# An encoder step with 16 attention heads: which projection blocks are computed beside the attention

## The chip, the cores and the metric

The kernel is one program on one core of a Trainium2 chip. The metric is the device time in microseconds (us). The engines are named as in the profile: PE is TensorE (matmuls; PEld its weight loads), DVE is VectorE, ACT is ScalarE, POOL is GpSimd, and SP issues most of the transfers.

## The reference, cut to what matters

Two groups of requests, 512 prompt rows and 8 x 16 sample rows, go through one layer together, 640 rows in all:

```python
h = rms_norm(x, g_pre)
(sq, sk, sv, sg, bq, bk, bv, bg, mq, mg, gsb, gbd, gmm) = split(h @ w_in)   # 13312 columns
o_sb = stick_breaking(sq, sk, sv)        # 6 heads of 128; sigmoid and a running product
o_bd = band_attention(bq, bk, bv, bias)  # 6 heads; softmax with a bias
o_mm = memory_attention(mq, mk, mv)      # 4 heads; softmax over 256 memory rows
merged = (sigmoid(gsb) * ((o_sb * silu(sg)) @ w_up_sb)
          + sigmoid(gbd) * ((o_bd * silu(bg)) @ w_up_band)
          + sigmoid(gmm) * ((o_mm * silu(mg)) @ w_up_mem))
y = x + rms_norm(merged @ w_out, g_post)
```

The sample rows attend to cached keys and values as well, 512 rows per stream (256 for the memory heads).

## The kernel before, in words

The 13312 columns of `w_in` are 104 blocks of 128 columns: 24 for the six stick-breaking heads (q, k, v, gate), 24 for the six band heads, 8 for the four memory heads (q, gate), and 48 merge gates (3 x 16). Every product is done as three matmuls of split operands (high x high, high x low, low x high), so a plain block is 16 k-steps x 3 x 2 halves of the rows = 96 matmuls of 128x320. Two blocks can also be done together with seven half-size products in place of eight: such a pair (`block_pair`) is 7 x 8 x 3 = 168 matmuls.

The stages are, in time: the memory projection and the norm of x; four plain gate blocks (`gate`); 34 pairs; the attention with 32 plain blocks beside it; the three up-projections (`up`); the output projection with the last norm.

- The pairs are 12 for the band heads' q, k, v and gate, whose results go to DRAM (`put_raw`, issued by POOL, tensors `raw_d`), and 22 for merge gates, whose sigmoids go to DRAM (`put_gate`, issued by ACT, tensors `sig_d`). Between the pairs SP lays the cached keys out anew in DRAM (`cut_keys`, tensors `keys_d`).
- In the attention the heads follow `ORDER`. 0 to 5 are stick-breaking, 6 to 11 band, 12 to 15 memory heads. A stick-breaking or memory head computes its own blocks as plain ones (`transposed`, `head_g`, both over `x_proj`), 24 + 8 = 32 blocks; a band head loads its four (`loaded`). The generators of a head are run in turns (`interleave`): the prompt's attention, the sample's scores, and the sample's output of the head before.
- The prompt's attention of a head has four query blocks. For each, PE computes scores `s`; DVE and ACT turn them into weights `b` (softmax for band and memory heads, `softmax`; two sigmoids and a running product for stick-breaking heads, `stick`); PE transposes `b` into `tp`; ACT and DVE split `tp` into `wth` and `wtl`; PE multiplies these with the values into `o`.
- The plain blocks take their weights in half blocks of 512 KB (`load_w`, tile `wr`), which ACT and DVE split into `wh` and `wl`.

The order of the program's text is not the order on the engines: a scheduler orders all instructions of each engine when the program is built, by its own estimate of their times. `tc.issue_after(x)` holds what stands in it behind the instruction x on the same engine; `x_proj` uses it to keep the plain blocks in the order of the text. Once built, each engine runs its list strictly in that order, and waits at an instruction whose inputs are not there.

ACT holds one set of functions at a time. Where an exponential follows a sigmoid, or the other way round, an ACT_TABLE_LOAD stands between them in ACT's list; the build puts it there.

Of the kernel before, what the change touches and what calls it, by code (L numbers as in the profile page):

```python
# [8 lines left out]
F32 = mybir.dt.float32  # L9
F32R = mybir.dt.float32r  # L10
AF = mybir.ActivationFunctionType
ALU = mybir.AluOpType
# [4 lines left out]
P = 128  # L17
# [18 lines left out]
LATE = 4  # L36

FIRST = 4


ORDER = (0, 6, 1, 7, 12, 2, 8, 3, 9, 13, 4, 5, 14, 15, 10, 11)

# [4 lines left out]
def stream_step_kernel(  # L47
# [46 lines left out]

    raw_d = [[dpool.tile([P, NT], F32, name=f"raw_d{n}_{h}") for h in range(6)] for n in range(4)]
    sig_d = [dpool.tile([P, NT], F32, name=f"sig_d{i}") for i in range(3 * KB)]
# [77 lines left out]

    def proj(w, col, kn, src, acc, half=8, back=False):

        starts = range(0, kn, half)
        for i0, k0 in enumerate(reversed(starts) if back else starts):
            n = min(half, kn - k0)
            wh, wl = load_w(w[k0 * P:(k0 + n) * P, col:col + P].rearrange("(k p) c -> p k c", p=P), [P, n, P])  # L180
            for k in range(n):
                bh, bl = src(k0 + k)
                first, last = i0 == 0 and k == 0, i0 == len(starts) - 1 and k == n - 1
                for a, b, f, l in ((wh, bh, True, False), (wh, bl, False, False), (wl, bh, False, True)):
                    for s in range(2):
                        PE.matmul(acc[:, s, :HF], a[:, k], b[s],  # L186
                                  start=first and f, stop=last and l)

    def x_proj(col, acc):

        nonlocal last_mm, back
        with tc.issue_after(last_mm or last_on(PE)):
            proj(w_in, col, KB, x_src, acc, back=back)
        last_mm, back = last_on(PE), False

# [175 lines left out]
    def loaded(n, h):  # L371
        t = pa.tile([P, NT], F32, tag=f"l{n}", name=f"l{n}", bufs=2 if n == 0 else 1)
        SP.dma_start(t, raw_d[n][h])
        return t

    def transposed(col, n, raw):

        if raw is not None:
            return loaded(n, raw)
        acc = new_acc()  # L380
        x_proj(col, acc)
        t = pa.tile([P, NT], F32, tag=f"l{n}", name=f"l{n}", bufs=2 if n == 0 else 1)
        ACT.copy(halves(t), acc[:, :, :HF])
        return t

    def head_g(col, raw=None):
        sg = stg.tile([P, NT], F32, tag="sig", name="sg")
        if raw is not None:
            SP.dma_start(sg, raw_d[3][raw])
            return sg  # L390
        acc = new_acc()
        x_proj(col, acc)
        ACT.activation(halves(sg), acc[:, :, :HF], AF.Sigmoid)
        DVE.tensor_tensor(halves(sg), acc[:, :, :HF], halves(sg), op=ALU.mult)  # L394
        return sg
# [205 lines left out]
    def causal_head(i):  # L601

        kind, h, c0 = ("sb", i, C_SB) if i < 6 else ("bd", i - 6, C_BD)
        cv = (cache_sb_v, cache_band_v)[i // 6]
        kp, vp, ks, vs = (tokens(t)[:, h] for t in ((sbk_p, sbv_p, sbk_s, sbv_s), (bdk_p, bdv_p, bdk_s, bdv_s))[i // 6])
        strip, strips = None, None
        if kind == "bd":
# [10 lines left out]
            strips = (st[:, TS:], st2)  # L618
        raw = h if kind == "bd" else None
        sg = head_g(c0 + 2304 + h * P, raw)  # L620
        vt = transposed(c0 + 1536 + h * P, 2, raw)
        nat = pa.tile([P, 4, P], F32, tag="nat", name="nat")
# [5 lines left out]
        vn = natural_new(vt, vs, "vn")  # L628
        qt = transposed(c0 + h * P, 0, raw)
        kt = transposed(c0 + 768 + h * P, 1, raw)  # L630
        v = split_v(nat)
# [18 lines left out]
    def mem_head(h):  # L650
        vn = pa.tile([P, 4, P], F32, tag="nat", name="vnm")[:, :2]
        kn = pa.tile([P, NT], F32, tag="l2", name="knm")[:, :NMEM].rearrange("p (t e) -> p t e", t=2)
        for t, o in ((kn, 0), (vn, 512)):
            SP.dma_start(t, kv_d[:, o + h * P:o + (h + 1) * P].rearrange("(t p) e -> p t e", p=P))
        qt = transposed(C_MM + h * P, 0, None)
        sg = head_g(C_MM + 512 + h * P)
        tp = bank("tp")
# [24 lines left out]

    def gate(i):
        acc = new_acc()
        x_proj(C_GATE + i * P, acc)
# [29 lines left out]
    for i in range(FIRST):  # L715
        gate(i)
        third.append(sums(2 * i))
# [122 lines left out]
    with tc.tile_pool(name="att", bufs=1, reuse_waits="tile") as pa:  # L840
        qm, wTm = zero_padded(4)

        rest = iter(())
        for h in ORDER:
            prompt, score, out = causal_head(h) if h < 12 else mem_head(h - 12)
            interleave(rest, prompt, score)
            rest = out
        interleave(rest)
    xs.close()
# [19 lines left out]
    def up(i):  # L869
# [132 lines left out]
```

## Time and profile before

| | us |
|---|---|
| median of 3 runs (2084.43 to 2088.02) | 2087.05 |
| the profiled execution, its own time | 2088.03 |
| its span in the profile | 2086.3 |
| PE busy | 2045.1 (98%) |
| DVE busy | 1104.4 (53%) |
| ACT busy | 817.0 (39%) |
| POOL busy | 570.1 (27%) |

A row of groups gives line, engine, operation, out<-in by the program's names, shapes and count, then busy time, mean ns of one, and idle time of the engine before them with what ended it. PE's busy time is a union of matmuls whose ends are modelled; what PE loses is seen in its waits and in the granted clock (PEclk). A row of waits reads: who <- for whom: us in total, times, longest us.

### The profile page before, as it was taken

To read this page: it belongs to the slowest core of one execution; us is meant where nothing else is said; L and a number is where in the kernel's file an instruction comes from. 1 tells how busy PE (TensorE), PEld (TensorE's weight loads), DVE (VectorE), ACT (ScalarE), POOL (GpSimd) and SP (SyncE) were. 2 spreads that over 40 slices of the span, in tenths; PEclk is the share of its full clock that TensorE was granted. 3 is DMA by queue.
4 is the path that set the end of the run, shared out by engine and by line. 5 is a ranking of instruction groups with operands and counts; after the bars stand their busy time and mean duration, and the time that the engine had idled before them with its cause. 6 is when DMAs were issued, how large, how long until landed. Compare 5 with 4: busy or idle time off the path is not lost.

```text
span 2086.3 us, 35971 instructions
## 1 busy us (share of the span) xinstructions
PE 2045.1 (98%) x13997; PEld 1934.7 (93%) x13997; DVE 1104.4 (53%) x1804; ACT 817.0 (39%) x1567; POOL 570.1 (27%) x539
## 2 busy tenths in 40 slices
PE   7999999999999999999999999989999999999998
PEld 5999999999999999999999799979998899998886
DVE  6875555555555555555355645555455665542234
ACT  6543444444444444444233333333334232322221
POOL 1155455664444444441010101010100015330000
PEclk9999999999999999999999999989999999999999
DMA  7656665565556655645557646653556875532225
GB/s 264 213 145 157 166 162 146 140 154 147 147 138 162 164 140 136 154 127 167 154 157 214 186 131 197 195 177 109 164 156 216 242 205 172 166 124 72 81 89 214
DMA packets 556889, 336.49 MB, mean 161 GB/s; under 512 B 271761, under 2 KB 507297, under 8 KB 555181
## 3 DMA queue, kind: packets, MB, share of 16 engines
q1 hardware_dynamic: 542942, 294.53, 50.9%
q0 software_dynamic: 6864, 23.93, 3.3%
q10 hardware_dynamic: 6912, 15.73, 2.0%
q8 instruction: 110, 1.80, 0.4%
q14 instruction: 61, 0.50, 0.1%
HBM read 288.75 MB, written 76.35 MB: 175 GB/s over the span
## 4 chain that ended last, share of the span: by engine, by line
PE 91%; DMA 2%; issue 2%; DVE 2%; POOL 1%; ACT 1%; SPq 0%; DVEq 0%; POOLq 0%; ACTq 0%
PE q L748 40%; PE acc L186 32%; PE ya L171 4%; PE ya L172 3%; PE ya L173 3%; PE s L528 2%; POOL merged L888 1%; PE o L587 1%; DMA kc<-keys_d 1%; DMA wr<-in_w_mem_kv_dram 1%; PE tp L458 1%; PE o L171 1%; DMA or<-osg_d 0%; PE o L172 0%; PE o L173 0%
## 5 line engine op out<-in xcount | busy, mean ns | idle before, releaser
L115 DVE TENSOR_TENSOR wl<-wr,wh 128x512 fp32r<-128x512 f32 (+1 forms) x524 | 383.0, 734 | 384.0 <-ACT wh L114 373.3
L114 ACT CAST wh<-wr 128x512 fp32r<-128x512 f32 (+1 forms) x524 | 316.7, 608 | 607.4 <-PE acc L186 250.5
L115 DVE TENSOR_TENSOR wl<-ws,wh 128x512 fp32r<-128x512 f32 x272 | 231.3, 852 | 232.4 <-ACT wh L114 231.8
L748 PE MATMUL q<-xh,wh 128*128 128x320 f32 x1088 | 336.2, 309 | 0.0
L748 PE MATMUL q<-xh,wl 128*128 128x320 f32 x1088 | 336.2, 309 | 0.0
L748 PE MATMUL q<-xl,wh 128*128 128x320 f32 x1088 | 336.1, 309 | 0.0
L114 ACT CAST wh<-ws 128x512 fp32r<-128x512 f32 x272 | 168.9, 622 | 271.3 <-PE q L748 230.3
L186 PE MATMUL acc<-xh,wl 128*128 128x320 f32 x1152 | 269.9, 312 | 0.0
L186 PE MATMUL acc<-xh,wh 128*128 128x320 f32 x1152 | 267.5, 311 | 1.2 <-DVE sg L394 1.2
L186 PE MATMUL acc<-xl,wh 128*128 128x320 f32 x1152 | 267.7, 311 | 0.0
L748 PE MATMUL q<-th,wl 128*128 128x320 f32 x816 | 252.2, 309 | 0.0
L748 PE MATMUL q<-th,wh 128*128 128x320 f32 x816 | 252.1, 309 | 0.0
L748 PE MATMUL q<-tl,wh 128*128 128x320 f32 x816 | 252.1, 309 | 0.0
L748 PEld LDWEIGHTS q<-xh,wl 128*128 128x128 f32 x1088 | 204.6, 188 | 0.0
L748 PEld LDWEIGHTS q<-xl,wh 128*128 128x128 f32 x1088 | 204.5, 188 | 0.0
L748 PEld LDWEIGHTS q<-xh,wh 128*128 128x128 f32 x1088 | 204.5, 188 | 0.0
L186 PEld LDWEIGHTS acc<-xh,wh 128*128 128x128 f32 x1152 | 193.2, 188 | 8.1 <-issue 5.4
L186 PEld LDWEIGHTS acc<-xl,wh 128*128 128x128 f32 x1152 | 193.5, 188 | 7.6 <-issue 7.5
L186 PEld LDWEIGHTS acc<-xh,wl 128*128 128x128 f32 x1152 | 193.9, 188 | 2.3 <-issue 1.8
L741 POOL TENSOR_TENSOR ws<-wr 128x512 f32<-128x512 f32 x102 | 150.7, 1491 | 93.7 <-DVE wl L115 77.1
L748 PEld LDWEIGHTS q<-th,wl 128*128 128x128 f32 x816 | 153.2, 188 | 0.2 <-DVE wl L115 0.2
L748 PEld LDWEIGHTS q<-tl,wh 128*128 128x128 f32 x816 | 153.2, 188 | 0.0
(239 smaller groups left out, 3262.2 us busy)
## 6 DMA issues: line engine op xcount, KB each, us to landing
wr<-in_w_in_dram SPq DMA_DIRECT2D x208, 512.0 KB, 4.7
kc<-keys_d SPq DMA_DIRECT2D x48, 512.0 KB, 5.0
wr<-in_w_out_dram SPq DMA_DIRECT2D x32, 512.0 KB, 3.7
sig_d<-sig ACTq DMA_DIRECT2D x48, 320.0 KB, 5.3
sig<-sig_d SPq DMA_DIRECT2D x48, 320.0 KB, 3.7
keys_d<-in_cache_sb_k_dram SPq DMA_DIRECT2D x96, 128.0 KB, 4.5
keys_d<-in_cache_band_k_dram SPq DMA_DIRECT2D x96, 128.0 KB, 4.5
vc<-in_cache_sb_v_dram SPq DMA_DIRECT2D x48, 256.0 KB, 5.5
```

The costliest lines, as they stand in the source:

```text
L114: ACT.copy(hi, src)
L115: DVE.tensor_tensor(lo, src, hi.bitcast(F32), op=ALU.subtract)
L171: PE.matmul(out, ah, bh, start=start, stop=False)
L172: PE.matmul(out, ah, bl, start=False, stop=False)
L173: PE.matmul(out, al, bh, start=False, stop=stop)
L186: PE.matmul(acc[:, s, :HF], a[:, k], b[s], start=first and f, stop=last and l)
L458: PE.transpose(tp[:, kb * P:(kb + 1) * P], b[:, kb * P:(kb + 1) * P], ident)
L528: return PE.matmul(s[32 * j:32 * j + 32, :nc_], qm[:, j, par * 32:par * 32 + 32], kts[j], start=par == 0, stop=par == 1, tile_position=(0, ...
L587: PE.matmul(o[32 * j:32 * j + 32, :P], l, r, start=i == 0, stop=i == len(steps) - 1, tile_position=(0, 32 * j))
L741: eng.tensor_tensor(o, a[c], b[c], op=op)
L748: PE.matmul(bank_, a[:, k], b[:, k], start=first and k == 0 and n == 0, stop=k == KH - 1 and n == 2, skip_group_check=not first)
L888: POOL.tensor_tensor(merged[:, j], merged[:, j], sig, op=ALU.add)
```

## The change

It has five parts.

1. All 16 heads load their blocks from DRAM. The pairs are now 12 for the band heads, 12 for the stick-breaking heads, 4 for the memory heads, and 6 for merge gates: 34 again.
2. The 32 plain blocks beside the attention are merge gates. `x_proj` becomes a generator (`x_proj_steps`) that hands over after each half block. One half block is run ahead of each head, and `beside(PER)` runs four more in turns with the head's own generators; 64 half blocks are used up within the 13th head.
3. The gate of a head has a tile of its own (`sg`, two buffers), and q has one buffer in place of two.
4. `ORDER` has the memory heads later: 0, 6, 1, 7, 2, 8, 3, 9, 4, 12, 5, 13, 14, 10, 15, 11.
5. In the up-projections the tiles `or` and `sig` share four buffers in place of five.

The number of pairs (34) and of plain blocks (36) is the same, and so are the heads' own matmuls.

```diff
-ORDER = (0, 6, 1, 7, 12, 2, 8, 3, 9, 13, 4, 5, 14, 15, 10, 11)
+ORDER = (0, 6, 1, 7, 2, 8, 3, 9, 4, 12, 5, 13, 14, 10, 15, 11)
...
-    def x_proj(col, acc):
+    def x_proj_steps(col, acc):
 
         nonlocal last_mm, back
-        with tc.issue_after(last_mm or last_on(PE)):
-            proj(w_in, col, KB, x_src, acc, back=back)
-        last_mm, back = last_on(PE), False
+        steps, back = proj_steps(w_in, col, KB, x_src, acc, 8, back), False
+        for _ in range(KB // 8):
+            with tc.issue_after(last_mm or last_on(PE)):
+                next(steps)
+            last_mm = last_on(PE)
+            yield
...
-        t = pa.tile([P, NT], F32, tag=f"l{n}", name=f"l{n}", bufs=2 if n == 0 else 1)
+        t = pa.tile([P, NT], F32, tag=f"l{n}", name=f"l{n}")
         SP.dma_start(t, raw_d[n][h])
         return t
...
-        sg = head_g(c0 + 2304 + h * P, raw)
-        vt = transposed(c0 + 1536 + h * P, 2, raw)
+        sg = head_g(i)
+        vt = loaded(2, i)
...
-        qt = transposed(c0 + h * P, 0, raw)
-        kt = transposed(c0 + 768 + h * P, 1, raw)
+        qt, kt = loaded(0, i), loaded(1, i)
...
-    pairs = [(C_BD + 768 * n + h * P, put_raw(n, h)) for n in range(4) for h in range(0, 6, 2)]
-    pairs += [(C_GATE + i * P, put_gate(i)) for i in range(FIRST, 3 * KB, 2)]
+    gates = [*range(KB), *range(2 * KB, 3 * KB), *range(KB, 2 * KB)]
+    pairs = [(c + 768 * n + h * P, put_raw(n, i + h)) for c, i in ((C_BD, 6), (C_SB, 0)) for n in range(4) for h in range(0, 6, 2)]
+    pairs += [(C_MM + 512 * n + h * P, put_raw(3 * n, 12 + h)) for n in range(2) for h in range(0, 4, 2)]
+    pairs += [(C_GATE + i * P, put_gate(i)) for i in gates[FIRST:-BESIDE:2]]
...
-        for h in ORDER:
+        left = gates[-BESIDE:]
+        steps = (None for i in left for _ in gate_steps(i))
+
+        def beside(n):
+
+            for _ in range(n):
+                yield
+                next(steps, None)
+                yield
+                yield
+
+        for n, h in enumerate(ORDER):
+            next(steps, None)
             prompt, score, out = causal_head(h) if h < 12 else mem_head(h - 12)
-            interleave(rest, prompt, score)
+            interleave(rest, prompt, score, beside(PER))
             rest = out
+        for _ in steps:
+            pass
         interleave(rest)
...
-        r = po.tile([P, NT], F32, tag="sig", name="or", bufs=5)
+        r = po.tile([P, NT], F32, tag="sig", name="or", bufs=4)
...
-        sig = po.tile([P, NT], F32, tag="sig", name="sig", bufs=5)
+        sig = po.tile([P, NT], F32, tag="sig", name="sig", bufs=4)
```

Three places show the order on the engines; a number behind a name tells one tile from the next. The first is PE's list in band head 9, from the transposes of the first query block's weights (`b_14797`) to the first product with the values. In the kernel before these rows follow each other:

```order
L458 MATMUL tp_14847<-ident_66,b_14797 128x128 x4
L593 MATMUL t3_14856<-ident_66,on_14845 128x128
L171 MATMUL s_14860<-kh_14745,qh_14738 128x384
L172 MATMUL s_14860<-kl_14746,qh_14738 128x384
L173 MATMUL s_14860<-kh_14745,ql_14739 128x384
L458 MATMUL tp_14875<-ident_66,b_14864 128x128 x3
L171 MATMUL o_14883<-wth_14789,vh_14734 128x256
```

The same place in the changed kernel (second query block, weights `b_14821`):

```order
L174 MATMUL s_14817<-kh_14640,qh_14633 128x384
L175 MATMUL s_14817<-kl_14641,qh_14633 128x384
L176 MATMUL s_14817<-kh_14640,ql_14634 128x384
L189 MATMUL acc_14754<-xh11_80,wh_14860 128x320
...
L189 MATMUL acc_14960<-xh01_76,wh_14963 128x320
L454 MATMUL tp_14832<-ident_66,b_14821 128x128 x3
L189 MATMUL acc_14960<-xl00_75,wh_14963 128x320
```

Before, the scores `s_14860` are followed at once by the transposes of the weights made of them, and those at once by the product that needs their split; now 49 matmuls of a gate block stand between the scores and the transposes, and 24 between the transposes and the product.

The second place is ACT's list in the same band head. Before, from the first query block's exponential to the third's:

```order
L569 COPY wTm_10604<-tp_14778 128x16x2x16
L481 ACT_TABLE_LOAD
L481 ACTIVATE b_14797,sm_14799<-b_14797,sm_14799 128x512
L590 COPY on_14845<-o_14784 128x128
L114 CAST wth_14789<-tp_14847 128x4x128
L481 ACTIVATE b_14864,sm_14866<-b_14864,sm_14866 128x384
L114 CAST wth_14789<-tp_14875 128x3x128
L393 ACT_TABLE_LOAD
L393 ACTIVATE sg_15412<-acc_15413 128x640
L481 ACT_TABLE_LOAD
L481 ACTIVATE b_14909,sm_14911<-b_14909,sm_14911 128x256
```

Now, from the same exponential on:

```order
L565 COPY wTm_10634<-tp_14673 128x16x2x16
L477 ACT_TABLE_LOAD
L477 ACTIVATE b_14692,sm_14694<-b_14692,sm_14694 128x512
...
L477 ACTIVATE b_14821,sm_14823<-b_14821,sm_14823 128x384
L117 CAST wh_15053<-wr_15047 128x512
L680 ACT_TABLE_LOAD
L680 ACTIVATE sig_14957<-acc_14754 128x640
L674 DMA sig_d18_197<-sig_14957 128x640
L117 CAST wth_14684<-tp_14832 128x3x128
L117 CAST wh_15111<-wr_15109 128x512
L477 ACT_TABLE_LOAD
```

In each of the heads 6 to 9 a merge gate's sigmoid now stands between the second and third exponentials, and another ahead of the sample's, each with a table load on either side; before, only heads 7 and 9 have one sigmoid each among their exponentials (that of a memory head's gate). From the end of the pairs to the last softmax ACT's list has 15 table loads before and 37 now: 19 ahead of an exponential, 14 ahead of a gate's sigmoid, 4 ahead of a stick-breaking head's sigmoid.

The third place is SP's list at the start of the attention. Before, behind the last load of the pairs:

```order
L141 DMA wr_10786<-in_w_in_dram 128x8x128
L514 DMA kc_11144<-keys_d0_90 128x1024
L514 DMA kc_11171<-keys_d0_90 128x1024
L141 DMA wr_10860<-in_w_in_dram 128x8x128
L609 DMA strip_11278<-rext_d_82 128x512
```

and now:

```order
L144 DMA wr_10988<-in_w_in_dram 128x8x128
L390 DMA sg_10696<-raw_d3_0_163 128x640
L385 DMA l2_10698<-raw_d2_0_151 128x640
L385 DMA l0_10713<-raw_d0_0_123 128x640
L385 DMA l1_10715<-raw_d1_0_139 128x640
L510 DMA kc_10764<-keys_d0_90 128x1024
```

Head 0's gate, v, q and k are loaded first there, ahead of its keys. On PE, 48 matmuls of the first gate block stand between the last pair and the transposes of v (`l2`); before, two plain blocks and 27 matmuls of a third stood ahead of the first such transposes.

More of the change, by code (lines that the diff above doesn't have):

```diff
@@ L36 @@
 LATE = 4
+BESIDE = 32
+PER = 4
 FIRST = 4
-ORDER = (0, 6, 1, 7, 12, 2, 8, 3, 9, 13, 4, 5, 14, 15, 10, 11)
+ORDER = (0, 6, 1, 7, 2, 8, 3, 9, 4, 12, 5, 13, 14, 10, 15, 11)
 C_SB, C_BD, C_MM, C_GATE = 0, 3072, 6144, 7168
@@ L93, in stream_step_kernel @@
     b12_d = dpool.tile([P, KH, HF], F32, name="b12_d")
-    raw_d = [[dpool.tile([P, NT], F32, name=f"raw_d{n}_{h}") for h in range(6)] for n in range(4)]
+    raw_d = [[dpool.tile([P, NT], F32, name=f"raw_d{n}_{h}") if n in (0, 3) or h < 12 else None for h in range(16)]
+             for n in range(4)]
     sig_d = [dpool.tile([P, NT], F32, name=f"sig_d{i}") for i in range(3 * KB)]
@@ L173, in mm3, with proj_steps @@
         PE.matmul(out, al, bh, start=False, stop=stop)
-    def proj(w, col, kn, src, acc, half=8, back=False):
+    def proj_steps(w, col, kn, src, acc, half=8, back=False):
         starts = range(0, kn, half)
@@ L187, in proj @@
                                   start=first and f, stop=last and l)
-    def x_proj(col, acc):
-        nonlocal last_mm, back
-        with tc.issue_after(last_mm or last_on(PE)):
-            proj(w_in, col, KB, x_src, acc, back=back)
-        last_mm, back = last_on(PE), False
+            yield
+    def proj(*args):
+        for _ in proj_steps(*args):
+            pass
+    def x_proj_steps(col, acc):
+        nonlocal last_mm, back
+        steps, back = proj_steps(w_in, col, KB, x_src, acc, 8, back), False
[4 more added lines that the diff above has]
+            yield
     def x_src(k):
@@ L371, in loaded, with head_g @@
     def loaded(n, h):
-        t = pa.tile([P, NT], F32, tag=f"l{n}", name=f"l{n}", bufs=2 if n == 0 else 1)
+        t = pa.tile([P, NT], F32, tag=f"l{n}", name=f"l{n}")
         SP.dma_start(t, raw_d[n][h])
         return t
[L376 to L394, printed above, removed]
+    def head_g(h):
+        sg = pa.tile([P, NT], F32, tag="sg", name="sg", bufs=2)
+        SP.dma_start(sg, raw_d[3][h])
         return sg
@@ L601, in causal_head @@
     def causal_head(i):
-        kind, h, c0 = ("sb", i, C_SB) if i < 6 else ("bd", i - 6, C_BD)
+        kind, h = ("sb", i) if i < 6 else ("bd", i - 6)
         cv = (cache_sb_v, cache_band_v)[i // 6]
@@ L618, in causal_head @@
             strips = (st[:, TS:], st2)
-        raw = h if kind == "bd" else None
-        sg = head_g(c0 + 2304 + h * P, raw)
-        vt = transposed(c0 + 1536 + h * P, 2, raw)
+        sg = head_g(i)
+        vt = loaded(2, i)
         nat = pa.tile([P, 4, P], F32, tag="nat", name="nat")
@@ L654, in mem_head @@
             SP.dma_start(t, kv_d[:, o + h * P:o + (h + 1) * P].rearrange("(t p) e -> p t e", p=P))
-        qt = transposed(C_MM + h * P, 0, None)
-        sg = head_g(C_MM + 512 + h * P)
+        qt, sg = loaded(0, 12 + h), head_g(12 + h)
         tp = bank("tp")
@@ L681, in put_sig, with gate_steps @@
         ACT.dma_start(sig_d[i], sig)
-    def gate(i):
+    def gate_steps(i):
         acc = new_acc()
-        x_proj(C_GATE + i * P, acc)
+        yield from x_proj_steps(C_GATE + i * P, acc)
         sig = stg.tile([P, NT], F32, tag="sig", name="sig")
@@ L715, in stream_step_kernel @@
     for i in range(FIRST):
-        gate(i)
+        for _ in gate_steps(i):
+            pass
         third.append(sums(2 * i))
@@ L843, in stream_step_kernel @@
         rest = iter(())
-        for h in ORDER:
+        left = gates[-BESIDE:]
[5 more added lines that the diff above has]
+                yield
+                yield
+        for n, h in enumerate(ORDER):
+            next(steps, None)
             prompt, score, out = causal_head(h) if h < 12 else mem_head(h - 12)
-            interleave(rest, prompt, score)
+            interleave(rest, prompt, score, beside(PER))
             rest = out
+        for _ in steps:
+            pass
         interleave(rest)
```

## The prediction

> **What bounds the kernel now.** I read the page first, then a table of stretches, then PE's waits, and last one softmax in order of time.
>
> ```profile
> span 2086.3 us, 35971 instructions
> ...
> PE   7999999999999999999999999989999999999998
> ...
> PEclk9999999999999999999999999989999999999999
> ```
>
> PE is at work from end to end, with one dent (slice 28, in busy share and in clock). Cut at the stages, and in the attention (974 to 1640) at the dents:
>
> ```profile
> core 0: us, PE busy (x) PEld busy (x) DVE busy (x) ACT busy (x) POOL busy (x), PEclk, DMA share, GB/s
> 136.00:452.00 316.00, 316.00 (x2157) 316.00 (x2156) 168.13 (x217) 133.09 (x239) 183.96 (x138) 1.00 0.60 152
> 452.00:974.00 522.00, 522.00 (x3559) 521.78 (x3559) 282.82 (x365) 240.03 (x428) 235.58 (x167) 1.00 0.56 144
> 974.00:1085.00 111.00, 111.00 (x752) 104.62 (x751) 49.01 (x79) 33.24 (x67) 7.93 (x21) 1.00 0.57 168
> 1085.00:1200.00 115.00, 109.30 (x926) 100.17 (x925) 66.55 (x134) 44.47 (x92) 10.71 (x30) 1.00 0.71 208
> 1200.00:1380.00 180.00, 179.44 (x1420) 166.72 (x1420) 94.27 (x185) 66.70 (x145) 16.10 (x44) 1.00 0.57 168
> 1380.00:1425.00 45.00, 36.45 (x280) 32.18 (x279) 26.63 (x58) 16.35 (x36) 4.06 (x11) 0.85 0.59 181
> 1425.00:1585.00 160.00, 160.00 (x1299) 150.18 (x1298) 79.74 (x165) 58.44 (x131) 13.07 (x36) 1.00 0.50 141
> 1585.00:1640.00 55.00, 49.40 (x342) 42.02 (x341) 37.89 (x85) 22.29 (x50) 3.89 (x8) 0.97 0.90 289
> 1640.00:1858.00 218.00, 217.52 (x1628) 213.40 (x1624) 121.13 (x203) 68.40 (x135) 59.62 (x45) 1.00 0.60 175
> ```
>
> In the pairs (136 to 974) PE has no gap: 838 us for 5716 matmuls, 0.147 us each, and I use that price for every matmul of 128x320. All that can be lost or won lies in the attention. Two holes and the changeover to the up-projections lose there:
>
> - 1085 to 1200: 115.00 - 109.30 = 5.7 us idle;
> - 1380 to 1425: 45.00 - 36.45 = 8.55 us idle, and a granted clock of 0.85, which is 0.15 x 45 = 6.75 us more;
> - 1585 to 1640: 55.00 - 49.40 = 5.6 us idle and 0.03 x 55 = 1.65 us of clock.
>
> With 0.56 us of idle time in 1200 to 1380, the first two items hold 21.6 us together and the changeover 7.25. What PE waited for there:
>
> ```profile
> PE tp L458 <- DVE b L483: 7.3, 5, 3.2
> PE o L171 <- ACT wth L114: 2.7, 3, 1.5
> PE s L528 <- DVE sm L482: 2.4, 1, 2.4
> PE tp L568 <- DVE b L473: 2.0, 1, 2.0
> PE acc L186 <- DVE sm L480: 2.0, 1, 2.0
> PE acc L186 <- ACT oh L114: 1.7, 2, 1.1
> PE acc L186 <- DVE sg L394: 1.2, 1, 1.2
> ```
>
> No wait is on a weight or on a key. PE waits for softmax weights, for their split, and for the DVE work queued with them, and it does so in the places where the order gives it nothing else: in the first excerpt of the order, zero matmuls stand between the scores and the transposes that need their weights, and that is the 3.2 us wait. Counted over the whole order of before, this cover (matmuls between scores and transposes, at 0.147 us, with the narrow ones at what they take) is under 3.5 us in four places, with 1.3, 2.8, 2.9 and 0.0 us, all beside heads 7 and 9; between transposes and product it is zero in three places, two of them in the holes. Head 9 stands between heads 3 and 13, where few blocks were left to put in.
>
> **What a softmax needs.** This is the first query block of band head 8, in order of time:
>
> ```profile
> 1300.18 0.40 PE L173 MATMUL s<-kh,ql 128*128 128x512 f32 x1
> 1300.69 0.69 DVE L452 SCALAR_TENSOR_TENSOR b<-s,strip 128x512 f32<-128x512 f32 x1 [0.48 <-PE s L173]
> 1301.41 0.69 DVE L478 TENSOR_REDUCE sm<-b 128x1 f32<-128x512 f32 x1
> 1302.28 0.62 ACT L114 CAST wh<-wr 128x512 fp32r<-128x512 f32 x1 [1.88 <-PE acc L186]
> 1302.91 1.28 ACT L481 ACT_TABLE_LOAD   x1
> 1304.21 0.72 ACT L481 ACTIVATE b<-b,sm 128x512 f32<-128x512 f32 x1
> 1305.26 0.49 DVE L483 TENSOR_SCALAR b<-b,sm 128x512 f32<-128x512 f32 x1
> 1305.89 0.63 PE L458 MATMUL tp<-ident,b 128*128 128x128 f32 x4 [0.56 <-DVE b L483]
> ```
>
> Scores end at 1300.58, transposes start at 1305.89: 5.3 us, of which 0.8 went to a weight split that stood ahead on ACT and 1.28 to the table load. So the chain is 4.5 us with a table load in it and about 3.2 without, plus what stands ahead on ACT or DVE. PE's cover here was 4.75 us, hence a wait of 0.56. This is the yardstick for the change.
>
> **The change part by part**, against the profiled execution's own 2088.03 us (the span of 2086.3 and 1.7 around it; 1.0 above the median of 2087.05).
>
> *Pairs and plain blocks, PE.* 34 pairs and 36 plain blocks before and after: 0. The 16 pairs that become raw ones (stick-breaking and memory) issue their stores on POOL in place of ACT, and 10 more blocks multiply by their sigmoid on POOL. What hides that: the band pairs already do all this in 136 to 452, where POOL is busy 184 of 316 us (58%, against 45% in the gate pairs) and PE is 316.00 of 316. Cost 0; without that cover it would be POOL's time per pair, 6% of it more.
>
> *The holes.* In the changed order no cover between scores and transposes is under 4.0 us while plain blocks last, save one of 3.2 at their very end; between transposes and product it is at least 3.2 us in all places but that same one. The two holes go: -21.6 us. The bound on the other side is that none of it goes, if something else holds PE there.
>
> *Changeover.* The uncovered place that remains is the last block of memory head 14, where the up-projections start. The pattern is the one of before (1585 to 1640), with the DMA share at 0.90 there: 7.25 us stay, 0. Bounds -7.25 and +3.
>
> *ACT's list and its table loads.* The rows of 975 to 1640:
>
> ```profile
> L383 ACT COPY l<-acc 128x640 f32<-128x640 f32 x22 | 15.2, 690 | 0.3 <-PE acc L186 0.3
> L481 ACT ACT_TABLE_LOAD x8 | 10.3, 1283 | 9.1 <-DVE sm L478 9.0
> L393 ACT ACTIVATE sg<-acc 128x640 f32<-128x640 f32 x10 | 7.0, 704 | 5.3 <-issue 4.0 <-DMA osg_d<-sg 1.3
> L393 ACT ACT_TABLE_LOAD x4 | 5.1, 1283 | 0.1
> L445 ACT ACT_TABLE_LOAD x3 | 3.8, 1283 | 0.1
> ```
>
> The 22 copies (15.2 us) and 10 sigmoids (7.0) of the heads' blocks go; 32 gate sigmoids x 0.704 = 22.5 us, 32 issues x 0.33 = 10.7 us (the row of ACT's issues stands below) and 37 - 15 = 22 table loads x 1.283 = 28.2 us come. ACT goes from 219 us in the 611 us of 974 to 1585 (the sum of those rows) to about 258, some 42%: not a bound. What counts is the load inside a softmax: the idle time of 9.0 us ahead of L481's loads shows that they wait for the maximum (`sm`), so each of the 19 loads ahead of an exponential lengthens its chain by 1.28. Against covers: first query blocks of four band heads 4.6 us against 4.5, third ones 5.5 against 4.5 or less, samples 6.5, memory heads 4.0 to 6.2. Most fit, with little to spare where a weight split stands ahead. Bounds: 0, and 28.2 if each of the 22 added loads reached PE whole. I take 0.2 us for each of 19, +4 us, near the covered end, since the one case in a place of the same cover cost 0.56 with a split ahead, and softmaxes with 4.9 us of cover or more cost nothing.
>
> The Trainium skill, "ScalarE: Activation LUTs", section "What ACT_TABLE_LOAD costs", puts a switch at about 2.66 us, 1.28 of load and 1.38 of draining, and its rules for authors say to do all of one set before switching. The load's 1283 ns agrees; the draining does not show here, where the exponential starts 0.02 us behind the load. By the page 22 switches would be an estimated 58.5 us of ACT, and 19 chains each up to 1.38 us longer: up to 26 us more, or 2098.
>
> *Start of the attention.* Head 0's v is now needed 48 x 0.147 = 7.05 us behind the last pair, and the transposes of k, q's split and the first scores some 4 us later. The loads:
>
> ```profile
> 974.52 0.82 SPq L514 DMA_DIRECT2D kc<-keys_d  x2
> ```
>
> ```profile
> sig<-sig_d SPq DMA_DIRECT2D x48, 320.0 KB, 3.7
> ...
> l<-raw_d SPq DMA_DIRECT2D x18, 320.0 KB, 4.2
> ```
>
> ```profile
> L681 ACTq DMA_DIRECT2D sig_d<-sig x48: 326/334/393, 97.5 to 975.6; - x48
> ```
>
> Before, SP's first load into the attention's buffers left at 974.5, as the pairs ended; in its place the gate's load leaves, 0.4 us later v's, then q's and k's. With 4.2 us to landing v is there at about 979 against a need at 981.5. Bounds 0 and 4 (k late behind three loads); I take +1.
>
> *Transfers.* 32 loads and 32 stores of 320 KB more in the attention are 21 MB on top of 104 MB (the rows of 974 to 1585, length times GB/s), so the DMA share, 0.58 in their mean, goes to roughly 0.70. The stretch of 1640 to 1858 runs with 0.60 and 1085 to 1200 with 0.71, and PE waits for no transfer in either. Bounds 0 and 16 (1 us for each head whose loads come late); I take +1. SP and the heads' q with one buffer are in this. The weights behind these loads on SP have three buffers of 512 KB, 3 x 48 matmuls or 21 us ahead.
>
> *Four buffers in the up-projections*: a block of the memory branch is 24 x 0.147 = 3.5 us, four are 14 us, against 3.7 us to land: 0.
>
> Sum: -21.6 + 4 + 1 + 1 = -15.6 us, 2088.0 to 2072.4; against the median I say 2072.
>
> **Rivals.**
>
> *Table loads on the path (slower).* A rule by which every switch is paid: the place is heads 6 to 9 and the memory heads, where each gate sigmoid splits a run of exponentials. For it: the loads wait for `sm`, and 0.56 us was lost in the one place with a cover as in the change. Against: loads before with 4.9 us of cover cost nothing. If each of the 22 costs 1.28 us, PE loses 28.2 in place of 4: 2072 + 24 = 2096. The mean loss per added load from which the change gains nothing is (15.6 + 4) / 22 = 0.9 us.
>
> *The holes move (about the same).* Head starts wait for their four loads, bunched with eight loads of cached values: 1 us for each of 16 heads is 16 us, 2087; at half of it 2079. For it: a share of 0.90 in the changeover. Against: PE's waits on transfers are nil there, too.
>
> *The changeover closes as well (faster still).* 2072 - 7 = 2065. For it: the plain blocks no longer have to end with a head's own block. Against: the order still has one uncovered product there, behind a sigmoid and a load.
>
> **How the numbers follow.** The forecast, 2066 to 2079: 0.56. Changeover closed, about 2065 and below: 0.13. Holes move, 2079 to 2090: 0.19, of which 0.08 is still faster. Table loads paid, 2090 to 2100: 0.12. I take 0.2%, 4.2 us, as what a measurement can tell: faster 0.56 + 0.13 + 0.08 = 0.77, same 0.11, slower 0.12. The range 2062 to 2090 leaves out the table loads' case and a little below.
>
> **What would show it.** Right: stretches of 100 us in the attention with PE idle under 1 us each, the clock at 1.00 outside the changeover, 41 table loads in all, waits of PE on `b` of 0 to 0.6 us in heads 6 to 9, and pairs that still take 838 us. Wrong: waits of `tp` on `b` of 1.3 us behind loads (table loads), PE or DVE waiting for `l`, `kc` or `vc` (transfers), a gap at 981 (start), or idle time of PE in the pairs (POOL's stores).

## The result, and the profile after

The changed kernel takes 2061.31 us, the median of four runs (2060.58 to 2064.45), against 2087.39 us of the kernel before beside it: a ratio of 0.9881, 95% interval 0.9864 to 0.9898. That is 26 us, or 1.2%, faster; the forecast was 15 us (2072), and the time lies 0.7 us below the low end of its range (2062 to 2090) and 4.7 us below the 2066 to 2079 that the forecast itself was given.

From the page of the kernel after, the span and two rows of the span in 40 slices (tenths of busy time, tenths of the granted clock):

```profile
span 2058.9 us, 36034 instructions
...
PE   8999999999999999999999999999999999999998
...
PEclk9999999999999999999999999999999999999999
```

The dent of slice 28 is gone from both rows. The same stretches as before, moved by what the stages moved:

```profile
core 0: us, PE busy (x) PEld busy (x) DVE busy (x) ACT busy (x) POOL busy (x), PEclk, DMA share, GB/s
136.00:452.00 316.00, 316.00 (x2157) 316.00 (x2156) 171.33 (x217) 132.18 (x237) 183.18 (x139) 1.00 0.62 154
452.00:975.00 523.00, 523.00 (x3565) 522.60 (x3564) 294.47 (x365) 227.58 (x407) 277.05 (x208) 1.00 0.54 143
975.00:1085.00 110.00, 109.53 (x879) 103.69 (x881) 61.39 (x113) 48.37 (x96) 12.01 (x32) 1.00 0.82 252
1085.00:1200.00 115.00, 114.23 (x902) 105.89 (x903) 60.92 (x114) 47.46 (x93) 12.30 (x34) 1.00 0.75 226
1200.00:1380.00 180.00, 178.34 (x1459) 166.97 (x1456) 98.19 (x186) 79.08 (x152) 19.08 (x50) 1.00 0.70 212
1380.00:1565.00 185.00, 185.00 (x1443) 174.52 (x1442) 84.27 (x196) 76.01 (x156) 10.24 (x29) 1.00 0.58 179
1565.00:1640.00 75.00, 73.33 (x591) 67.22 (x590) 51.47 (x113) 28.98 (x65) 4.22 (x11) 1.00 0.91 285
1640.00:1831.00 191.00, 189.78 (x1369) 184.42 (x1368) 109.63 (x178) 59.87 (x116) 58.25 (x40) 1.00 0.58 169
```

The pairs are as full as before (316.00 of 316, 523.00 of 523). Beside the attention, 975 to 1565, PE now lacks 0.47 + 0.77 + 1.66 + 0 = 2.9 us, and the clock stays at 1.00 through it and through the changeover. What PE waits for from 975 to 1700 (us in total, times, longest):

```profile
PE o L174 <- ACT wth L117: 1.5, 1, 1.5
PE tp L454 <- ACT on L586: 1.4, 3, 0.5
PE tp L454 <- DVE b L479: 0.9, 3, 0.3
PE acc L189 <- ACT oh L117: 0.8, 1, 0.8
PE tp L454 <- DVE b L469: 0.6, 1, 0.6
```

The waits of 2.0 to 3.2 us are gone. Seven small ones of `tp` are left, 2.9 us together, each at a head's first query block. In all seven a table load stands between the scores and the transposes, and by the trace PE has 4.7 us of other matmuls there.

Where the 27.4 us between the two spans (2086.3 and 2058.9) lie follows from the starts of PE's matmuls. From the start of the program to the last pair: 0.8 longer. From there to the last plain block: 613.9 to 590.9, 23.0 shorter. From there to the first output product (`ya`): 270.3 to 264.9, 5.4 shorter. The rest is 0.1 longer. The prediction had given the changeover, the third part, nothing.

One more thing shows in PE's rows, which the prediction did not look at. The samples' scores against the cache are groups of four narrow matmuls (`s<-kt,qm`, weights 128x32, side by side in four column groups; the trace holds two records of each, so a whole group is x8). In time order on PE of the kernel after:

```profile
1084.94 1.07 PE L524 MATMUL s<-kt,qm 128*32 128x512 f32 x8
1085.94 0.56 PE L189 MATMUL acc<-xh,wh 128*128 128x320 f32 x2
...
1102.99 1.05 PE L524 MATMUL s<-kt,qm 128*32 128x512 f32 x4
1103.97 0.44 PE L454 MATMUL tp<-ident,b 128*128 128x128 f32 x2
...
1104.70 1.05 PE L524 MATMUL s<-kt,qm 128*32 128x512 f32 x4
1105.68 0.56 PE L189 MATMUL acc<-xh,wh 128*128 128x320 f32 x2
```

Four of them in a row hold PE for 1.00 us until the next matmul starts; two in a row hold it for 0.98. In the kernel before, where groups are also cut one and three:

```profile
1159.40 1.05 PE L528 MATMUL s<-kt,qm 128*32 128x512 f32 x2
1160.64 1.06 PE L528 MATMUL s<-kt,qm 128*32 128x512 f32 x6
1166.73 1.07 PE L528 MATMUL s<-kt,qm 128*32 128x512 f32 x8
```

One matmul is busy for 1.05 us, three for 1.06, four for 1.07. A group that the scheduler cuts in two by other matmuls costs twice. PE's list shows 34 such runs of the 512-column kind before and 30 now, for the same 24 groups.

The Trainium skill, "TensorE: Matmul & The Clock Gate", section "Part 3: Packing small matmuls — row/col tiling", gives the time of packed matmuls as that of one, plus about 4 ns for each further one. By the rows above three more cost 0.02 us, so the trace agrees.

### The profile page after: what moved, and what is told of

Its sections match the earlier page's. It is cut to its first block, busy times and chain, and to the rows that moved or that the text cites. A ratio compares the mean times of both kernels' runs of the same rounds, so it can differ in the third digit from the quotient of the medians.

```text
span 2058.9 us, 36034 instructions
## 1 busy us (share of the span) xinstructions
PE 2033.9 (99%) x13997; PEld 1928.4 (94%) x13997; DVE 1111.1 (54%) x1794; ACT 833.7 (40%) x1567; POOL 611.0 (30%) x581
## 4 chain that ended last, share of the span: by engine, by line
PE 93%; DMA 2%; issue 2%; DVE 1%; ACT 1%; POOL 1%; SPq 0%; DVEq 0%; ACTq 0%; POOLq 0%
PE q L742 41%; PE acc L189 33%; PE ya L174 4%; PE ya L176 4%; PE ya L175 4%; PE s L524 2%; PE o L583 1%; POOL merged L899 1%; PE tp L454 1%; DMA wr<-in_w_mem_kv_dram 1%; DMA or<-osg_d 1%; PE o L175 0%; PE o L176 0%; PE o L174 0%; PE s L175 0%
## 5 line engine op out<-in xcount | busy, mean ns | idle before, releaser
L118 DVE TENSOR_TENSOR wl<-wr,wh 128x512 fp32r<-128x512 f32 (+1 forms) x524 | 387.5, 744 | 360.1 <-ACT wh L117 356.9
L118 DVE TENSOR_TENSOR wl<-ws,wh 128x512 fp32r<-128x512 f32 x272 | 242.6, 896 | 223.4 <-ACT wh L117 222.8
L189 PEld LDWEIGHTS acc<-xh,wh 128*128 128x128 f32 x1152 | 192.5, 188 | 18.7 <-issue 17.2
L742 PEld LDWEIGHTS q<-th,wh 128*128 128x128 f32 x816 | 153.2, 188 | 0.2 <-ACT sig L759 0.2
```

Source lines behind the costliest of these rows:

```text
L118: DVE.tensor_tensor(lo, src, hi.bitcast(F32), op=ALU.subtract)
L189: PE.matmul(acc[:, s, :HF], a[:, k], b[s], start=first and f, stop=last and l)
L742: PE.matmul(bank_, a[:, k], b[:, k], start=first and k == 0 and n == 0, stop=k == KH - 1 and n == 2, skip_group_check=not first)
```

## The experiments

Times in the table are medians; the last five columns are of one profiled execution of each, in us: from the last pair to the first `ya`, and in this stretch the time of narrow scores, PE's waits of 0.1 us and more, the time lost to half clock (half the length of such stretches), and what remains of the first when the three are taken off.

| kernel | time, us | ratio to before (95%) | stretch | narrow | waits | clock | rest |
|---|---|---|---|---|---|---|---|
| before | 2085.9 to 2087.4 | 1 | 884.1 | 38.9 | 21.6 | 8.5 | 815 |
| changed | 2061.31 | 0.9881 (0.9864-0.9898) | 855.8 | 33.9 | 5.6 | 0 | 816 |
| e0_after, the same again | 2062.64 | 0.9889 (0.9876-0.9903) | 855.1 | 33.9 | 5.1 | 0 | 816 |
| e2_copy_gates | 2060.79 | 0.9883 (0.9868-0.9898) | 855.2 | 33.9 | 5.3 | 0 | 816 |
| e7_late_sigmoid | 2070.62 | 0.9927 (0.9914-0.9939) | 865.2 | 33.9 | 12.6 | 0 | 819 |
| e3_only_order | 2080.78 | 0.9974 (0.9963-0.9984) | 874.5 | 37.3 | 17.4 | 6.8 | 813 |
| e1_old_order | 2055.25 | 0.9854 (0.9840-0.9867) | 849.8 | 30.4 | 5.2 | 0 | 814 |
| e10_split | 2095.98 | 1.0045 (1.0032-1.0058) | 889.9 | 62.7 | 5.3 | 0 | 822 |
| e6_per3 | 2066.45 | 0.9904 (0.9888-0.9919) | 861.8 | 37.3 | 7.6 | 1.7 | 815 |
| e5_whole | 2078.32 | 0.9956 (0.9943-0.9968) | 872.8 | 29.5 | 21.9 | 8.5 | 813 |
| e14_e1_whole | 2060.12 | 0.9871 (0.9858-0.9885) | 854.6 | 29.9 | 8.2 | 3.4 | 813 |
| e8_double_loads | 2072.62 | 0.9927 (0.9915-0.9939) | 867.5 | 34.3 | 12.6 | 6.8 | 814 |
| e9_bufs5, one run | 2125.34 | - | 919.5 | 36.4 | 48.4 | 34.1 | 801 |
| e4_front, one run | 2160.59 | - | 953.4 | 33.2 | 68.4 | 52.9 | 799 |

Where a half-clock stretch begins inside a wait, the two columns count the same time twice: a little in e3, e5 and e8, much in the last two. Apart from these two, the rest is 813 to 822 us while the stretch itself runs from 850 to 890. Three terms carry the differences: narrow scores, waits, and the clock behind waits.

The changed kernel a second time, as the measure for the rest:

> The changed kernel once more, as the yardstick of the runs beside it on this chip: 2061 us, within 3.

Measured: 2062.64 us, the same gain within the intervals.

**Do the table loads cost anything?** The changed kernel with the 32 gates beside the attention stored as they are, without the sigmoid (part of the computation is left out), so that 26 of 41 table loads go:

```diff
-        ACT.activation(halves(sig), acc[:, :, :HF], AF.Sigmoid)
+        if i in gates[-BESIDE:]:
+            ACT.copy(halves(sig), acc[:, :, :HF])
+        else:
+            ACT.activation(halves(sig), acc[:, :, :HF], AF.Sigmoid)
```

> The 32 gates beside the attention are stored without their sigmoid (it is left out, so those gates are wrong in the result). ACT has 15 table loads in place of 41. Theory: the loads in the middle of a head fall beside other matmuls and cost nothing; only the first one of a head costs 0.3 to 0.6 us, and these remain: 2060 to 2061, the same within 0.1%. Rival, table loads: each of the 26 removed loads gives back 0.2 us or more, 2056 or less.

Measured: 2060.79 us. The table loads of 975 to 1700 in ACT's groups (busy time, mean ns, idle time before), of the changed kernel:

```profile
L477 ACT ACT_TABLE_LOAD x19 | 24.4, 1283 | 11.5 <-DVE sm L474 8.5 <-DVE sm L476 2.6
L680 ACT ACT_TABLE_LOAD x14 | 18.0, 1283 | 0.2
L441 ACT ACT_TABLE_LOAD x4 | 5.1, 1283 | 0.1
```

and of the one without sigmoids:

```profile
L477 ACT ACT_TABLE_LOAD x6 | 7.7, 1283 | 11.2 <-DVE sm L474 8.5 <-DVE sm L476 2.7
L441 ACT ACT_TABLE_LOAD x5 | 6.4, 1283 | 0.1
```

Thirteen of the 19 loads inside softmaxes are gone, and PE gains 0: 855.2 us of the stretch against 855.1 in the changed kernel that ran beside it, waits 5.3 against 5.1. Up to the last plain block it takes 590.0 us, against 590.3 beside it and 590.9 in the first profile of the changed kernel. But the loads that stay are those of the heads' first query blocks, and that is where PE's small waits are. In band head 7 of the kernel without sigmoids:

```profile
1127.26 1.28 ACT L477 ACT_TABLE_LOAD   x1 [2.25 <-DVE sm L474]
...
1130.24 0.63 PE L454 MATMUL tp<-ident,b 128*128 128x128 f32 x4 [0.31 <-DVE b L479]
```

So the run prices the loads in the middle of heads, nearly all that the change added, and not these. A load probably does cost something in a first query block: in the kernel before, those of heads 1 and 3 have no load, only 3.9 and 3.8 us of cover, and no wait. No run takes the load away there; in the changed kernel all seven such blocks together cannot cost more than the 2.9 us that PE waits in them.

The gates can also get their sigmoid later, where the up-projections load them, with the whole computation kept:

```diff
         with tc.issue_after(mark):
             SP.dma_start(sig, sig_d[g0 + j])
+        if g0 + j in gates[-BESIDE:]:
+            ACT.activation(sig, sig, AF.Sigmoid)
```

> As the one before, but the sigmoid of those 32 gates is taken where the up-projections load them (ACT, 128x640, 0.7 us each): nothing is left out. ACT has 22 table loads in place of 41. Theory: 2060 to 2063, the same within 0.1%, since ACT is busy a third of the time there. Rival, table loads: 2057 or less.

Measured: 2070.62 us, a miss. The attention is 2 us shorter (588.8 to the last plain block), but the part behind it is 11.6 us longer, 276.5 against 264.9. The largest group of PE's waits from 975 to 1850:

```profile
PE acc L189 <- DVE sig L904: 3.9, 6, 0.9
```

In the up-projections there is nothing to hide the sigmoid: the multiplication by it (L904) frees the accumulator, and PE waits for that. Beside the attention the sigmoid is in the cheaper place, table loads and all.

**Is it the cover, and which part of the change gives it?** Before with the new order of heads alone, without the blocks beside:

```diff
-ORDER = (0, 6, 1, 7, 12, 2, 8, 3, 9, 13, 4, 5, 14, 15, 10, 11)
+ORDER = (0, 6, 1, 7, 2, 8, 3, 9, 4, 12, 5, 13, 14, 10, 15, 11)
```

> The kernel before with the new ORDER alone. Cover theory: its order still has covers of 0.0 and 2.3 us in the band heads beside few blocks, and 32 narrow runs, so 2070 to 2086. Rival, head order (the later memory heads made the gain): 2061 to 2066.

Measured: 2080.78 us, 5 us faster than before and 18 to 20 us slower than the changed kernel. PE's waits from 975 to 1850:

```profile
PE o L171 <- ACT wth L114: 6.1, 4, 4.0
PE tp L458 <- DVE b L473: 5.8, 4, 3.5
PE tp L458 <- DVE b L483: 2.9, 2, 2.4
```

Holes stay and move (to 1230, 1320 and 1356), with half clock in and behind the first two. The order of heads is not what closes them. Only the hole at 1230 has no matmul at all between scores and transposes. In the other two a list is held by a store that still reads a tile, ACT's before the hole at 1320 and DVE's before the one at 1356:

```profile
1318.44 0.70 ACT L393 ACTIVATE sg<-acc 128x640 f32<-128x640 f32 x1 [3.60 <-DMA osg_d<-sg]
1350.54 0.71 DVE L638 STREAM_TRANSPOSE natk<-l 128x512 f32<-128x512 f32 x1 [2.54 <-DMA out_dram<-nat]
```

The changed kernel takes the first of these off ACT, since a head's gate is no longer computed there; no run tests that by itself.

The other way round, the changed kernel with the old order, the same line turned about:

```diff
-ORDER = (0, 6, 1, 7, 2, 8, 3, 9, 4, 12, 5, 13, 14, 10, 15, 11)
+ORDER = (0, 6, 1, 7, 12, 2, 8, 3, 9, 13, 4, 5, 14, 15, 10, 11)
```

> The changed kernel with ORDER of the kernel before. Cover theory (the gain is that plain blocks stand between scores and transposes in every head): all covers in its order are 3.0 us or more while plain blocks last, so 2061 to 2066. Rival, head order (the later memory heads make the gain, at the changeover above all): the 5 us won between the last plain block and the output projection come back, 2066 to 2068, and more if the holes were the memory heads' doing.

Measured: 2055.25 us, faster than the changed kernel and outside both expectations. The waits are as in the changed kernel (5.2 us), so the blocks beside each head's steps close the holes with either order. The further 6 us lie elsewhere: the narrow scores take 3.5 us less (26 runs of the 512-column kind, not 30), waits 0.4 less, and 2 us of the rest are not put down to anything. This is the fastest kernel of all that ran: the new order, part 4 of the change, costs 6 us beside the other parts.

Two kernels take the cover away at the end of the attention. Eight pieces between steps of a head use the blocks up after seven heads:

```diff
-PER = 4
+PER = 8
```

> Eight pieces of plain blocks between steps of a head in place of four, so that the 36 blocks are used up after about seven heads. Theory (cover between scores and transposes is what the change gains by): 25 softmaxes of the last heads stand with 0 to 3 us of matmuls where they need about 3.2 without a table load (none of these has one, since no gate is left: 27 loads in all against 41). Each loses about 2 us, 50 us together, and the clock falls beside the waits: 2110 to 2175. Rival (table loads are what a softmax costs, cover does not matter much): 14 loads fewer, so 2045 to 2062.

Measured: 2160.59 us. With five buffers in place of four in the up-projections,

```diff
-        sig = po.tile([P, NT], F32, tag="sig", name="sig", bufs=4)
+        sig = po.tile([P, NT], F32, tag="sig", name="sig", bufs=5)
```

(and the same for `or`), the up-projections stand behind the last head's steps in PE's list and not among them:

> The changed kernel with five buffers for or and sig in the up-projections, as before the change. With five the up-projections' pool has no room beside the attention's, and PE's list has them behind the last head: 14 softmaxes of the last three heads have a cover of 0 to 3.1 us. Cover theory: each waits for what is missing to about 3.5 us, some 35 us, and the clock falls to half in part of it, 2095 to 2140. Rival (the buffers do nothing): 2061.

Measured: 2125.34 us. The stretch of the last heads, of the first:

```profile
1565.00:1640.00 75.00, 44.30 (x353) 31.57 (x352) 43.99 (x106) 26.52 (x68) 8.86 (x22) 0.75 0.63 188
```

and of the second:

```profile
1565.00:1640.00 75.00, 44.48 (x322) 28.31 (x319) 44.65 (x111) 22.84 (x60) 6.51 (x16) 0.68 0.55 164
```

In both PE is idle for over 30 of 75 us, and the clock falls to 0.75 and 0.68. The kernel with eight pieces has 14 table loads fewer and is 98 us slower: cover is what a softmax needs. "Four buffers: 0" in the prediction was right as to time of transfers, and said nothing of what the buffer count does to the scheduler's order.

**The narrow scores.** If a run of narrow scores costs about 1 us whatever it holds, cutting every group in two must cost that much for each cut. The scores of a group are put out as two pieces of two, with a turn of other work between:

```diff
-                for j in range(3):
+                score(2)
+            yield
+            with tc.issue_after(last_on(PE)):
+                for j in range(2):
                     score(j)
```

> The changed kernel with each group of four narrow score matmuls (128x512 or 128x256, four column groups of PE side by side) written as two and two with a hand-over between. In PE's list the 512-wide groups stand in 56 runs in place of 30, the 256-wide in 14 in place of 9. Split theory (a run costs the same 0.98 us, or 0.57 for 256, whether it holds two or four): + 26 x 0.98 + 5 x 0.55 = 28 us, 2090. Rival (only cover matters; the covers stay at 4.0 us and more): 2060 to 2064.

Measured: 2095.98 us, 33 us slower than the changed kernel, with PE's waits unchanged at 5.3 us. The narrow scores take 28.8 us more, as the theory of the runs had it; 6 us of the rest come on top, for which there was no term. The group's row on PE (busy time, mean ns of one), before:

```profile
L528 PE MATMUL s<-kt,qm 128*32 128x512 f32 x192 | 36.0, 605 | 0.0
```

of the changed kernel, of the one with the old order, and of the one with the groups cut:

```profile
L524 PE MATMUL s<-kt,qm 128*32 128x512 f32 x192 | 31.8, 605 | 0.1
```

```profile
L524 PE MATMUL s<-kt,qm 128*32 128x512 f32 x192 | 27.6, 605 | 0.0
```

```profile
L524 PE MATMUL s<-kt,qm 128*32 128x512 f32 x192 | 58.8, 605 | 0.3 <-ACT e L477 0.3
```

The same 192 records, at the same 605 ns for one, keep PE busy for 36.0, 31.8, 27.6 and 58.8 us. Divided by the runs counted in PE's list, 34, 30, 26 and 56, that is 1.06, 1.06, 1.06 and 1.05 us: the number of runs explains the row.

Fewer pieces between steps move the narrow scores the other way, and leave blocks for the last heads:

```diff
-PER = 4
+PER = 3
```

> Three pieces of plain blocks between steps of a head in place of four, so that blocks last longer into the last heads. Least cover between scores and transposes 3.1 us, 43 table loads. Theory of the runs: 31 runs of 512 columns against 30, and 12 of 256 columns against 9 at 0.57 us, +2.7 us, and the waits as now or 1 to 2 us less: 2061 to 2066. Rival (the end of the plain blocks decides: with blocks left beside the last heads the part from the last block to the up-projections closes): 2050 to 2058.

Measured: 2066.45 us, just above what the theory of the runs gave, and not the rival's 2050 to 2058. Narrow scores cost 37.3 us against 33.9 (31 runs of 512 and 12 of 256 columns), waits 7.6 against 5.6, and 1.7 us of half clock come in. The part behind the last plain block falls by 12.7 us, to 252.2, but the part ahead of it grows by 18.7, to 609.6, since that is where the blocks now are: the end does not close for nothing.

A plain block given out whole, with two empty turns behind it, leaves fewer cuts:

```diff
             last_mm = last_on(PE)
-            yield
+        yield
+        yield
```

> A plain block is given out as one piece of 48 matmuls with two empty turns behind it, in place of three pieces of 16; the work is the same, 43 table loads against 41. Theory (a narrow score product costs 0.98 us for each unbroken run of it, whether one or four matmuls are in the run, beside the cover): 25 runs of 512 columns against 30, so 5 us less than the changed kernel from that, less 1 us for one place with 2.0 us of cover: 2056 to 2059. Rival (only waits count, and those are 5.6 us already): 2061 to 2064; cover theory alone with larger pieces: first query blocks stand with 4.17 to 4.46 us as now, so 2061 to 2064 too.

Measured: 2078.32 us, a clear miss, though the narrow scores did fall by 4.4 us (25 runs). What came in their place is a wait that the count of cover on PE cannot see. The largest group of PE's waits, 975 to 1700:

```profile
PE tp L455 <- DVE b L470: 12.6, 5, 3.4
```

and the DVE ahead of the longest, in order of time:

```profile
1291.78 0.71 DVE L633 STREAM_TRANSPOSE natk<-l 128x512 f32<-128x512 f32 x1 [5.68 <-DMA out_dram<-nat]
1292.41 0.65 DVE L118 TENSOR_TENSOR wl<-wr,wh 128x512 fp32r<-128x512 f32 x1
1292.98 1.22 DVE L468 TENSOR_TENSOR_SCAN e<-e 128x512 f32<-128x512 f32 x1
1294.23 0.69 DVE L470 TENSOR_TENSOR b<-b,e 128x511 f32<-128x511 f32 x1
```

The next head's `natk` and `nat` share one buffer. Its transpose waits 5.68 us until the store of v (`out_dram<-nat`) has left that buffer, and the running head's weights stand behind it on DVE. The row of this transpose has 28.8 us of idle time before it in this kernel. In the changed kernel it is

```profile
L632 DVE STREAM_TRANSPOSE natk<-l 128x512 f32<-128x512 f32 x10 | 7.1, 710 | 12.2 <-DMA out_dram<-nat 12.2
```

so the same wait is there too, hidden by covers and other work. Both edits together, old order and whole blocks:

> The changed kernel with the order of heads of the kernel before and plain blocks as whole pieces, so both edits that bring the runs of narrow scores together. 25 runs of 512 columns (26 with the old order alone, 30 in the changed kernel) and 8 of 256. Theory of the runs: no further gain over the old order alone, which took 2055.3, but for 1 us: 2053 to 2057, with up to 2 us of waits more where covers of 3.0 and 3.2 us stay. Rival (the two edits gain by other causes, each for itself): their gains add, 2048 to 2052.

Measured: 2060.12 us, slower than the old order alone: narrow scores 29.9 us against 30.4, but waits 8.2 against 5.2 and 3.4 of clock. Neither expectation held; a wait for `b` of 2.6 us at 1094.7 and one for `oh` of 2.6 us at 1565.8 came in.

**How much room do the transfers have?** Every load of a head's q, k, v and gate is issued twice, 18 MB more:

```diff
-        SP.dma_start(t, raw_d[n][h])
+        for _ in range(2):
+            SP.dma_start(t, raw_d[n][h])
```

(the gate's load likewise).

> The changed kernel with every load of a head's q, k, v and gate from DRAM issued twice, 56 loads or 18 MB more in the attention. Cover theory (transfers are hidden): 2061 to 2064. Rival, transfers (1 us a head for late loads): 2070 or more.

Measured: 2072.62 us, 10 us slower than the changed kernel. The time is the rival's, but the run does not show its mechanism, and the edit does more than add bytes: both copies write the same tile, and SP's list stands still until the first has landed. SP's waits from 975 to 1640:

```profile
SPq L386 <- DMA l<-raw_d: 71.6, 26, 5.0
```

The gates' loads add 49.8 us, and the changed kernel has no such waits. So the run does not tell how much bandwidth is left. PE waits for `kh` at the first head (3.9 us, at 1002.6), for weights at 1157.7 (3.05 us) and for `oh` at 1697.6 (2.9 us), with half clock in or behind the first two. Ahead of these two, on ACT:

```profile
1000.35 0.33 ACTq L676 DMA_DIRECT2D sig_d<-sig  x1
1000.72 0.27 ACT L411 COPY vn<-t 128x128 f32<-128x128 f32 x1 [7.11 <-DMA vc<-in_cache_sb_v_dram]
...
1149.23 0.70 ACT L682 ACTIVATE sig<-acc 128x640 f32<-128x640 f32 x1
1154.48 0.33 ACTq L676 DMA_DIRECT2D sig_d<-sig  x1
1154.89 1.28 ACT L479 ACT_TABLE_LOAD   x1 [4.96 <-DMA vc<-in_cache_band_v_dram]
```

Both times a gate's store holds ACT's list. The first was issued 6.7 us after the copy ahead of it had ended (993.6), and the splits of v and k stood behind it; the second was issued 4.5 us after the gate's sigmoid had ended (1149.9), and the exponential stood behind it. What exactly held these issues is not settled. The third wait is for a late load of the up-projections (`or`).

## Why the prediction was right, and by how much it was off

*Pairs, 0.* Right: 316.00 of 316 and 523.00 of 523; the last pair ends 0.8 us later, and between the kernels of this study the pairs begin anywhere from 135.0 to 138.9 us without a part in it of any edit.

*The holes, -21.6.* Right in size, and in mechanism for the most part. In 975 to 1565 PE's idle time went from 14.8 us (5.7 + 0.56 + 8.55) to 2.9, and the clock loss of 6.75 to 0: -18.7, against -15.6 with the prediction's own additions of 4 for table loads, 1 for the start and 1 for transfers. What remains are the waits at first query blocks. The experiments put the gain down to the cover: the order alone leaves 17.4 us of waits (6.4 of them behind the two stores), the blocks with either order leave about 5, and taking the cover away at one end costs 64 to 98 us.

But not all of the two holes was missing cover, and the reading "no wait is on a key" was not right. PE waited 0.7 us for `kt` itself, the cached keys as DVE transposes them. And the longest wait of the first hole stands at a softmax of head 7 with 6.6 us of cover; its maximum was queued on DVE behind keys whose load came late:

```profile
1176.82 0.77 DVE L524 STREAM_TRANSPOSE kt<-kc 128x256 f32<-128x256 f32 x2 [2.00 <-DMA kc<-keys_d]
...
1182.53 0.66 PE L458 MATMUL tp<-ident,b 128*128 128x128 f32 x4 [1.90 <-DVE b L483]
```

So some 2.3 of the 5.7 us (this wait and one of 0.4 for `kt`) go back to a transfer, in the very stretch of 1085 to 1200 that the prediction took as free of such waits. In the changed kernel DVE has no wait of over 0.4 us for these loads from 1085 to 1565. What that is worth beside the cover, no run separates.

*Table loads, +4 (bounds 0 and 28.2), and the slower rival of 2096.* Too high, and the slower rival is refuted. The step that failed is the 0.2 us for each of 19 loads, taken from one first query block in which a weight split stood ahead. The 13 of them in the middle of heads cost nothing that shows: with 26 loads taken away in all, the stretch is 855.2 us against 855.1. With the sigmoids moved behind the attention (22 loads in place of 41) the part up to the last plain block is 1.5 to 2.1 us shorter, which is the most that the loads there cost by these profiles. The loads at first query blocks stay in both runs; seven of them in the changed kernel are followed by waits of 0.3 to 0.6 us, and whether the load or something else in the chain makes these, no run settles. The Trainium skill, "ScalarE: Activation LUTs", section "What ACT_TABLE_LOAD costs", would have made ACT's list an estimated 58.5 us longer by draining as well as loading; its 1283 ns holds in every row here, and taking 26 loads away shows no price on PE.

*Start, +1, and transfers, +1.* Both were 0: of the 0.47 us idle in 975 to 1085, 0.43 is the wait at a first query block at 1083.5. The reason given for the start counted 4.2 us to landing; k took 7.8 us, and PE still lost nothing. The DMA share came out as estimated, 0.69 in 975 to 1565 against roughly 0.70.

*Changeover, 0 (bounds -7.25 and +3).* Wrong: it lost 7.25 us before, and now 1.67 us in 1565 to 1640 with the clock at 1.00. Of the product that waits for `wth`, 1.54 us are still there, as forecast; what went is a wait of 2.0 us on the next accumulator with half clock behind it, and smaller ones on `oh` and the gate. The kernels with the order alone and with the blocks alone have lost it too (263.9 and 264.3 us behind the last plain block, against 270.3), so it goes with the particular order of PE's list there. The changed kernel with whole blocks has 6.6 us of waits and 1.7 of half clock behind its last plain block again. That the rival "changeover closes" had this as its mechanism is so; why the scheduler placed that accumulator so is not settled.

*What had no term at all:* the narrow scores, -5.0 us (38.9 to 33.9). The prediction priced them "at what they take", as if that were fixed by their number. It is fixed by the number of unbroken runs, which any move of other matmuls changes; the order showed the runs, and nobody counted them.

Holes -18.7, changeover about -5, narrow scores -5.0, the later end of the pairs +0.8: -28 against the measured -27.4 of the spans. The forecast of 2072 had the first of these; with the changeover and the narrow scores right, and no price for loads, start and transfers, its own sum would have been 2088.0 - 21.6 - 5 - 5 = 2056, and 2059 with the 2.9 us of waits that stayed, against 2060.6 of the profiled execution. The measured time lies where the prediction had put the rival "changeover closes" (about 2065 and below, 0.13), not where it had put its own forecast (0.56). The direction and the main term were right; the gain was forecast too small because changeover and narrow scores stood at nothing, and loads, start and transfers at 6 us, where 2.9 us of waits stayed.

## What to carry to other kernels

Where one engine is full, look for the places where its list has no other work between a producer and its consumer, and count the cover there against the chain of the other engines, DVE's and ACT's own lists included: an instruction queued ahead that waits for a transfer (the store of the shared `nat` buffer, the load of the cached keys) spoils a cover that PE's list shows as ample. Count also how often an order cuts groups of narrow matmuls that share the array, since each cut costs as much as a whole group. And test a suspected price, such as a table load's, by taking the operation away before designing around it, and check that the run takes it away in the tight places too: here the loads with cover to spare cost nothing, and those without it stayed.

## What the runs showed of the hardware

A run of narrow fp32 matmuls (128x32 weights, 512 columns) holds PE for about 1 us whether it has one, two, three or four of them, and 1.06 us of busy time for each run fits four kernels to 1%.

A wait of PE can cost more than itself. From the end of the pairs to the first output product, of eleven waits of 2.0 to 2.9 us in the profiles of before, e3, e5, e14, e6 and e8, six had a stretch of 3.4 or 6.8 us at half clock that began in them or within 2 us of their end; of eight waits of 3.0 us and more, all had; of six between 1.2 and 1.95 us, one had. The Trainium skill, "TensorE: Matmul & The Clock Gate", section "Why this matters for your kernels", advises against idle gaps of over about 3 us between bursts; here the clock fell behind a gap of 2.0 us as well (at 1615.7 to 1617.7 of the kernel before).
